# Attention on Trainium2: the next pair's scores ahead of a pair's turning, and outputs multiplied by turned reciprocal sums

## The chip, the cores and the metric

The kernel runs on one core of one Trainium2 chip. The metric is the time of one execution on the device in microseconds (us), the median of several runs. The engines are TensorE (PE, its weight loads PEld), VectorE (DVE), ScalarE (ACT), GpSimd (POOL) and SyncE (SP), which issues the transfers.

## The reference

One layer of a decoder with 1024 tokens of width 1024 in float32. An RMSNorm and one input projection feed two mixers side by side: a gated DeltaNet with 4 heads of 128, and a dilated attention with 8 heads of 64. Their outputs are joined, projected, and added to the input; a gated MLP with a short convolution follows, and a last RMSNorm.

The change lies in the attention. Every query sees keys at three dilations, and the three branches are merged by their softmax denominators, which amounts to one softmax over all keys with weights:

```
DIL_PATTERNS = ((128, 1), (512, 4), (2048, 16))
num_tot = wts[0][..., None] * nums[0] + wts[1][..., None] * nums[1] + wts[2][..., None] * nums[2]
den_tot = wts[0] * dens[0] + wts[1] * dens[1] + wts[2] * dens[2]
out = num_tot / den_tot[..., None]
```

The kernel takes the branches' weights as logarithms in a mask `mk` and makes one softmax a query: exponentials, their sum, and a weighted sum of values divided by it.

## The kernel before, in words

**Who sets the order.** The kernel is written as streams (generators) that issue instructions; a planner, the class Weave, runs them. Every stream has a level; the lowest level that says it is ready goes next. A stream yields the time that it still has to wait, which `need` (L95) works out from the planner's own prices: for VectorE 0.07 us + 0.00105 us an element, for ScalarE 0.12 + 0.00085, and 0.28 more until others see the result (L148 to L152). A product notes its result as made 0.25 later (L88 to L93). The order of TensorE's instructions is fixed by this plan: every matmul and transpose carries an issue-order token. On the other engines a scheduler orders by readiness and priority; `uv` and `ua` are VectorE and ScalarE with a raised priority.

**The streams that matter.** `dense` (L478, level 9) makes the columns of the input projection: per column two halves of 8 x 3 products of 128x512, with raw weights split into a high and a low part first (`weight`, L211: whi on ScalarE, wlo on VectorE). The order of its columns is DENSE (L42): the queries and keys of attention (`a`) stand before the gates (`z`) of the other mixer. `attention` (L892, level 5) goes ahead of dense wherever it is ready, so dense fills. `out_proj` (L1072, level 8) begins when dense has ended.

**Attention.** Four head pairs (pi), for each two halves of the tokens (hh), for each two pairs of items (u = 0, 1 and 2, 3). An item is one block of 128 queries of two heads (e = 0, 1); n = 4 hh + u is its block. It has 128 or 256 near keys and 32 (n - 1) far ones, together wd = 128 to 448 columns. For a pair:

- `scores` (L904) takes two PSUM banks of the tag asc for the first item and two of atr for the second (each tag has two banks in all), and writes queries by keys into them.
- `softmax` (L929): for each head a fused add of the mask and minimum on VectorE (the reduce; it reads the bank and writes `sm`), then the exponential on ScalarE with its sum in `den`, then the reciprocal of `den` (128x2) and a scaling of the two rows of `sm` by it.
- `turn` (L945) transposes `sm` on TensorE into a fresh bank, of asc for the first item and atr for the second, in four steps (item by head). It waits for the bank and for `sm`, less a slack (TSLACK, 1.0 us and 0.6 us, L955). VectorE copies near columns to `pt`, ScalarE far ones to `pb`.
- `values` (L966) multiplies values by `pt` into the bank `po` of the half (tag ch), `merge_classes` (L975) adds those by `pb` when the half is complete, and `give` (L989) copies `po` to SBUF with its columns put back in order, and stores it.

`advance` (L1004) is the loop: it turns the older pair, issues the new pair's scores, and then the older pair's values. The loop at L1017 loads the next head pair when its second half begins, which waits for dense to have made its queries and keys (L1021).

**Slots.** SBUF tiles come from tags with a fixed number of buffers (SLOTS, L26). The tag `dv*` takes buffers of dv and dw in turn.

Of the kernel before, what the change touches and what calls it, by code (L numbers as in the profile page):

```python
# [7 lines left out]
F32 = mybir.dt.float32  # L8
F32R = mybir.dt.float32r
AF = mybir.ActivationFunctionType  # L10
OP = mybir.AluOpType
# [11 lines left out]
APART = 0.5  # L23
KSLACK = 1.0
EPS = 1e-6
SLOTS = {"kT": 2, "kU": 2, "dv": 2, "dw": 2, "kt": 4, "uy": 5, "qa": 4, "ev": 2, "go": 2, "Xa": 7, "Xb": 9}  # L26
TURNS = {"kT*": ("kT", "kU"), "dv*": ("dv", "dw"), "X": ("Xa",) * 7 + ("Xb",) * 9}
HTAGS = ("kU", "kU", "dw", "dw", "kt", "kt", "kt", "kt", "uy", "uy", "uy", "uy", "uy", "qa", "qa", "qa", "qa",
         "ev", "ev", "go", "go") + ("Xa",) * 7
R1TAGS = ("kU", "kt", "qa", "uy", "kt", "qa", "uy", "ev", "kU", "dw", "uy")  # L30
R2TAGS = ("kt", "kt", "uy", "uy", "qa", "qa", "ev", "go", "go", "dw", "Xa")
PTAGS = ("Xb",) * 9 + ("Xa",) * 2
TOKEN = "pe"
SLACK = 3.0
# [110 lines left out]
def hybrid_layer(tc, I, out):  # L145
# [22 lines left out]
    def A(name, tag, dt=F32, shape=(P, 1024)):  # L168
        if tag in TURNS:
            i = turns[tag] = turns.get(tag, -1) + 1  # L170
            tag = TURNS[tag][i % len(TURNS[tag])]
        return tile_(lp, shape, dt, name, tag, SLOTS[tag])

# [70 lines left out]
    def bank(tag, name="ps"):  # L244
        return tile_(pp_, (P, 512), F32, name, tag, 2)
# [544 lines left out]
    def chain(h):  # L790

        for i in range(H):
            yield from wv.until(("m", i))
            yield from wv.until(("v", i))
        d = G[h]
        kT, ktok, vtok, yt, ge, rq, gq, ke = [d[n] for n in ("kT", "ktok", "vtok", "yt", "ge", "rq", "gq", "ke")]
        if not ct:
            ct.append(A("ct", "uy", shape=(P, 8, P)))
        sts = ct[0][:, 2 * h:2 * h + 2, :]
        qa = chain_load(h, 0)  # L800
        ps = bank(("asc", "ch")[h // 2])
        ms = small("ms", 4)
        tg = str(h)
        st = None
        for c in range(NCH):
            cs = slice(c * P, (c + 1) * P)
            if c == 2 and h < 2:
                qb = chain_load(h, 1)
            if c == 3 and h >= 2:
                yield from wv.until(("c", h - 2, 3))  # L810
                qb = chain_load(h, 1)
            if c == 4:
                qa = qb
            qT, at = [qa[:, i, (c % 4) * P:(c % 4 + 1) * P] for i in range(2)]
            if c == 0:
                r = vtok[:, cs]
                yield wv.need(ps, vtok, yt)
            else:
                yield wv.need(ps, st, slack=HOP)
                mm(ps[:, 0:P], kT[:, cs], st, 0.215)  # L820
                r = tile_(sp, [P, P], F32, "r", "r" + tg, 1)
                uv.scalar_tensor_tensor(r, ps[:, 0:P], ngam[:, c, h:h + 1], vtok[:, cs], op0=OP.mult, op1=OP.add)
                yield wv.need(r, slack=HOP)
            mm(ps[:, P:2 * P], yt[:, c, :], r, 0.215)
            w = tile_(sp, [P, P], F32, "w", "w" + tg, 1)
            if c < NCH - 1:
                wke = tile_(sp, [P, P], F32, "wke", "r" + tg, 1)
                uv.tensor_scalar(wke, ps[:, P:2 * P], ke[:, c:c + 1], None, op0=OP.mult)
            ua.activation(w, ps[:, P:2 * P], AF.Copy)
            if c < NCH - 1:  # L830
                yield wv.need(wke, slack=HOP)
                mm(ps[:, 2 * P:3 * P], ktok[:, cs], wke, 0.215)
                sn = sts[:, c % 2, :]
                if c == 0:
                    uv.tensor_copy(sn, ps[:, 2 * P:3 * P])
                else:
                    uv.scalar_tensor_tensor(sn, st, ge[:, c:c + 1], ps[:, 2 * P:3 * P], op0=OP.mult, op1=OP.add)
            yield wv.need(w, qa, slack=HOP)
            po = yield from next_bank("atr")
            if c:  # L840
                mm(po[:, P:2 * P], qT, st, 0.215)
            mm(po[:, :P], at, w, 0.215)

            ua.activation(vtok[:, cs], po[:, :P], AF.Copy, scale=rq[:, c:c + 1])
            if c:
                uv.scalar_tensor_tensor(vtok[:, cs], po[:, P:2 * P], gq[:, c:c + 1], vtok[:, cs], op0=OP.mult,
                                        op1=OP.add)
            if c < NCH - 1:
                st = sn
            osq = tile_(sp, [P, P], F32, "osq", "osq", 1)  # L850
            ua.activation(osq, vtok[:, cs], AF.Square, accum_out=ms[:, c:c + 1])
            wv.done.add(("c", h, c))

        ve.tensor_scalar(ms, ms, 1.0 / 128, EPS, op0=OP.mult, op1=OP.add)
        rsqrt(ms, ms, NCH)
        po_.tensor_tensor(v8(vtok), v8(vtok), ms[:, :, None].to_broadcast([P, NCH, P]), op=OP.mult)
        wv.add(1, finish(h, vtok))
# [34 lines left out]
    def attention():  # L892
# [36 lines left out]
        def softmax(it):  # L929
            pss, wd = it.pop("ps"), it["wd"]  # L930
            sm = it["sm"] = A("sm", "dv*", shape=(P, 2, 512))
            mx = tile_(sp, [P, 4], F32, "mx", "mx", 4)
            mn, den = mx[:, :2], mx[:, 2:]
            for e in range(2):
                uv.tensor_tensor_reduce(out=sm[:, e, :wd], in0=pss[e][:, :wd], in1=mk[:, 448 - wd:], scale=-0.125,
                                        scalar=-NEG, op0=OP.add, op1=OP.min, accum_out=mn[:, e:e + 1])
            for e in range(2):
                ua.activation(sm[:, e, :wd], sm[:, e, :wd], AF.Exp, bias=mn[:, e:e + 1], scale=-1.0,
                              accum_out=den[:, e:e + 1])

            uv.reciprocal(den, den)
            for e in range(2):
                uv.tensor_scalar(sm[:, e, :wd], sm[:, e, :wd], den[:, e:e + 1], None, op0=OP.mult)

        def turn(pair):  # L945
            pts = A("pt", "dv*", shape=(P, 4, 256))
            for b, (it, tag) in enumerate(zip(pair, ("asc", "atr"))):
                sm, near, far = it["sm"], it["near"], it["far"]
                nf = -(-far // P)
                it["pt"] = []  # L950
                for e in range(2):
                    pt = pts[:, 2 * b + e, :]
                    it["pt"].append(pt)
                    pp = bank(tag)
                    yield wv.need(pp, sm, slack=TSLACK[b])  # L955
                    for i in range(near // P):
                        tp(pp[:, i * P:(i + 1) * P], sm[:, e, far + i * P:far + (i + 1) * P])
                    for i in range(nf):
                        tp(pp[:, near + i * P:near + (i + 1) * P], sm[:, e, i * P:(i + 1) * P])
                    uv.tensor_copy(pt[:, :near], pp[:, :near])  # L960
                    for i in range(nf):
                        rows = min(far - i * P, P)
                        ua.activation(it["pb"][e][:rows, it["u"], i, :], pp[:rows, near + i * P:near + (i + 1) * P],
                                      AF.Copy)

        def values(pair):  # L966
            yield wv.need(pair[0]["po"], *pair[0]["pt"], slack=-PSLACK)
# [21 lines left out]
        def give(g):  # L989
            po, hh = g["po"], g["hh"]  # L990
            oT = tile_(sp, [P, 512], F32, "oT", "t2", 2)
            ve.tensor_copy(oT.rearrange("p (n u c) -> p n c u", n=4, c=4),
                           po.rearrange("p (n c u) -> p n c u", n=4, c=4))
            if g["pi"] < 3 or hh == 0:
                sy.dma_start(mixer[4 + g["pi"]][:, half(hh)], oT)
            else:
                last["oT"] = oT
            if hh == 1:
                wv.done.add(("o", 4 + g["pi"]))
# [3 lines left out]

        def advance(pair):  # L1004
            done = pipe.pop() if pipe else None
            if done is not None:
                yield from turn(done)
            if pair is not None:
                yield from scores(pair)
                pipe.append(pair)  # L1010
            if done is not None:
                yield from values(done)
                if done[1]["u"] == 3:
                    yield from merge_classes(done[0]["g"])
                    give(done[0]["g"])

        for pi in range(4):  # L1017
            q, k, vn, vc = cur
            for hh in range(2):
# [7 lines left out]
                for t in pb:  # L1027
                    for rows, b in (((slice(96, 128), 0), (slice(32, 64), 1)) if hh else ((slice(32, 64), 0),)):
                        po_.memset(t[rows, 0 if b < hh else 2, b, :], 0.0)
                g = dict(po=po, pb=pb, hh=hh, pi=pi, vc=vc)  # L1030
                for u in (0, 2):
                    yield from advance([dict(n=4 * hh + i, u=i, q=q, k=k, vn=vn, po=po, pb=pb, g=g)
                                        for i in (u, u + 1)])
# [528 lines left out]
```

## Time and profile before

| What | us |
|---|---|
| median of 3 runs | 1223.81 |
| lowest and highest run | 1223.63, 1225.67 |
| the profiled execution's own time | 1230.37 |
| its span, first to last instruction | 1228.5 |
| busy in it: TensorE, VectorE, ScalarE | 1204.7, 948.3, 571.0 |
| attention stage, first scores to first output projection product | 329.8 to 484.7 |

The mean granted TensorE clock of the profiled execution is 0.993 of full speed. Times in the trace count from the span's start. In a row of groups come the line (often a helper's: L141 is an engine call with its raised or usual priority, L189 a matmul, L193 a transpose), the engine, the operation, the tiles written and read, the shapes, the count, then busy time, mean ns of one, and the idle time in front with what ended it. In windows there are busy time and count for each engine, then the granted clock (PEclk), the share of the DMA engines and GB/s. A tile's rows have shortest, median and longest duration in ns, and the first and last start. In a timeline stand start, duration, engine, line and operation, with the idle time in front in brackets. Matmuls overlap one another: the spacing of their starts, not their duration, is what one costs.

### The profile page before, as it was taken

Reading aid. Unit: us, or ns where it says so; the run is one execution under the profiler, and the core shown is the slowest. Engines: PE = TensorE matmul, PEld = TensorE weight load, DVE = VectorE, ACT = ScalarE, POOL = GpSimd, SP = SyncE. Lnnn points to the kernel's source line nnn. Section 1 sums busy time; section 2 is a strip of 40 time slices with the busy share of each in tenths; the row PEclk is TensorE's granted clock in tenths of the full one; section 3 lists DMA queues with packets and bytes.
Section 4 is the critical chain, followed back from the end, with each engine's and each line's share of the span. In section 5 each row is a group of like instructions: output and inputs, shape, how many; then the busy total and the mean of one; then the engine's idle time right before and its main releaser. Section 6 shows DMA issues by size and latency. Waiting matters only on the chain.

```text
span 1228.5 us, 17935 instructions
## 1 busy us (share of the span) xinstructions
PE 1204.7 (98%) x6848; PEld 993.7 (81%) x6848; DVE 948.3 (77%) x1522; ACT 571.0 (46%) x1115; POOL 51.5 (4%) x58
## 2 busy tenths in 40 slices
PE   9999999999999999999999999999999999999996
PEld 7878887888877777788788888888888878787885
DVE  7675964566476778567888988889888889898875
ACT  7393344356344345555545445444444553344541
POOL 0211010003100000000000000000000000000000
PEclk9999999999999999999999999999999999999998
DMA  7325252345723303344123132231221496455523
GB/s 232 104 76 166 86 142 82 121 132 154 231 84 104 121 27 118 140 138 154 52 86 103 52 103 84 71 103 54 101 93 62 134 370 238 166 164 175 193 86 138
DMA packets 85799, 154.80 MB, mean 126 GB/s; under 512 B 21168, under 2 KB 36304, under 8 KB 85712
## 3 DMA queue, kind: packets, MB, share of 16 engines
q1 hardware_dynamic: 85712, 153.64, 38.8%
q8 instruction: 54, 0.88, 0.3%
q14 instruction: 33, 0.27, 0.1%
HBM read 117.68 MB, written 35.93 MB: 125 GB/s over the span
## 4 chain that ended last, share of the span: by engine, by line
PE 81%; DVE 8%; DMA 5%; issue 2%; ACT 2%; SPq 0%; POOLq 0%; POOL 0%; DVEq 0%; ACTq 0%
PE ps L189 42%; PE pa L189 19%; PE pc L189 9%; PE dw L189 8%; DMA wd<-in_wd 3%; PE ps L193 3%; DVE pr L139 2%; DMA r<-upark 2%; DVE wd L139 1%; DVE x1h L139 1%; DVE kT L139 1%; PE warm L189 1%; ACT dec L139 1%; DMA wst<-in_wu 0%; DVE sm L141 0%
## 5 line engine op out<-in xcount | busy, mean ns | idle before, releaser
L189 PE MATMUL dw<-pr 128*128 128x512 f32 (+1 forms) x984 | 213.4, 378 | 3.5 <-DVE x1h L139 2.3
L189 PEld LDWEIGHTS dw<-pr 128*128 128x128 f32 x984 | 176.1, 188 | 39.7 <-DVE x1h L139 4.4
L189 PE MATMUL ps<-xhi,whi 128*128 128x512 f32 x384 | 160.2, 417 | 0.0
L189 PE MATMUL ps<-xhi,wlo 128*128 128x512 f32 x384 | 150.4, 392 | 0.0
L189 PE MATMUL ps<-xlo,whi 128*128 128x512 f32 x384 | 150.2, 391 | 0.0
L189 PE MATMUL pa<-T,pair 128*128 128x512 f32 x528 | 128.7, 393 | 1.3 <-ACT u L139 1.3
L189 PEld LDWEIGHTS pa<-T,pair 128*128 128x128 f32 x528 | 100.2, 190 | 22.5 <-ACT u L139 1.6
L189 PEld LDWEIGHTS ps<-xhi,wlo 128*128 128x128 f32 x384 | 72.2, 188 | 15.7
L189 PEld LDWEIGHTS ps<-xhi,whi 128*128 128x128 f32 x384 | 72.5, 189 | 14.9 <-issue 2.6
L189 PEld LDWEIGHTS ps<-xlo,whi 128*128 128x128 f32 x384 | 72.7, 189 | 11.2
L139 ACT ACTIVATE u<-pa 128x512 f32<-128x512 f32 x44 | 26.3, 598 | 110.4 <-PE pa L189 110.4
L139 DVE SCALAR_TENSOR_TENSOR y<-xu,fcw,y 128x1023 f32<-128x1023 f32 (+1 forms) x44 | 56.4, 1281 | 25.7 <-ACT y L139 25.6
L139 ACT ACTIVATE whi<-wst 128x1024 fp32r<-128x1024 f32 (+2 forms) x42 | 43.0, 1023 | 68.8 <-PE ps L189 62.4
L189 PE MATMUL pc<-T,S 128*128 128x512 f32 x264 | 63.4, 389 | 0.0
L189 PE MATMUL pa<-B,A 128*128 128x512 f32 x264 | 63.4, 389 | 0.0
L189 PE MATMUL pc<-B,pair 128*128 128x512 f32 x264 | 63.4, 389 | 0.0
L189 PE MATMUL pa<-T,S 128*128 128x512 f32 x264 | 63.4, 389 | 0.0
L141 ACT ACTIVATE sm<-sm,mx 128x128 f32<-128x128 f32 (+7 forms) x64 | 35.5, 555 | 58.8 <-DVE mx L141 58.8
L139 DVE TENSOR_TENSOR wst<-wst 128x512 f32<-128x512 f32 x88 | 60.5, 688 | 0.8
L189 PE MATMUL ps<-B,pair 128*128 128x512 f32 x252 | 60.5, 389 | 0.0
L139 DVE TENSOR_TENSOR wlo<-wst,whi 128x1024 fp32r<-128x1024 f32 (+2 forms) x42 | 49.4, 1177 | 13.2 <-ACT whi L139 13.0
L139 ACT ACTIVATE pr<-wd 128x1024 fp32r<-128x1024 f32 x33 | 34.9, 1059 | 51.9 <-PE dw L189 23.1
(238 smaller groups left out, 2363.7 us busy)
## 6 DMA issues: line engine op xcount, KB each, us to landing
wst<-in_wu SPq DMA_DIRECT2D x44, 512.0 KB, 3.7
wd<-in_wd SPq DMA_DIRECT2D x44, 512.0 KB, 4.2
upark<-y SPq DMA_DIRECT2D x22, 512.0 KB, 3.7
wst<-in_wi SPq DMA_DIRECT2D x21, 512.0 KB, 3.7
r<-upark SPq DMA_DIRECT2D x11, 512.0 KB, 8.1
r<-upark SPq DMA_DIRECT2D x22, 256.0 KB, 7.1
wa<-in_wd SPq DMA_DIRECT2D x22, 256.0 KB, 2.7
wst<-in_wv SPq DMA_DIRECT2D x8, 512.0 KB, 3.7
```

The lines of the kernel that those rows point to most:

```text
L139: return getattr(eng, op)(*a, **kw)
L141: return getattr(eng, op)(*a, **kw)
L189: tc.stamp_issue_order_token(nc.tensor.matmul(dst, lhs, rhs, start=start, stop=stop, **kw).ins, TOKEN)
L193: tc.stamp_issue_order_token(nc.tensor.transpose(dst, src, ident).ins, TOKEN)
```

## The change

Two things in attention, and slots that go with them.

*The order.* `advance` issues the new pair's scores first, then turns the older pair, then its new step `spread`, then its values.

*The division.* `softmax` leaves the exponentials unscaled and keeps `den`. `turn` makes, for each item, a 128x128 tile `rd` whose columns are the reciprocal of the item's two sums, 64 columns for each head. `spread` transposes `rd` into a bank `rb` (tag ch, one for each half), so that every output element has its reciprocal at its own place; once the half is complete, ScalarE copies the bank to `rT`. `give` multiplies `po` by `rT` in place of the plain copy.

*Slots.* `pt` goes from `dv*` to a tag `ux` with one buffer, which `uy` gives up; the tags of some tiles of the MLP follow.

```
-SLOTS = {"kT": 2, "kU": 2, "dv": 2, "dw": 2, "kt": 4, "uy": 5, "qa": 4, "ev": 2, "go": 2, "Xa": 7, "Xb": 9}
+SLOTS = {"kT": 2, "kU": 2, "dv": 2, "dw": 2, "kt": 4, "uy": 4, "ux": 1, "qa": 4, "ev": 2, "go": 2, "Xa": 7, "Xb": 9}
...
-            ct.append(A("ct", "uy", shape=(P, 8, P)))
+            ct.append(A("ct", "ux", shape=(P, 8, P)))
...
-
-            uv.reciprocal(den, den)
-            for e in range(2):
-                uv.tensor_scalar(sm[:, e, :wd], sm[:, e, :wd], den[:, e:e + 1], None, op0=OP.mult)
+            it["den"] = den
...
         def turn(pair):
-            pts = A("pt", "dv*", shape=(P, 4, 256))
+            pts = A("pt", "ux", shape=(P, 4, 256))
             for b, (it, tag) in enumerate(zip(pair, ("asc", "atr"))):
-                sm, near, far = it["sm"], it["near"], it["far"]
+                sm, near, far, den, u = it["sm"], it["near"], it["far"], it["den"], it["u"]
+                rd = tile_(sp, [P, P], F32, "rd", ("r0", "r1", "w0", "w1")[u], 1)
+                uv.reciprocal(rd.rearrange("p (e d) -> p e d", e=2), den[:, :, None].to_broadcast([P, 2, 64]))
+                it["rd"] = rd
...
+        def spread(pair):
+            g = pair[0]["g"]
+            yield wv.need(g["rb"], *[it["rd"] for it in pair])
+            for it in pair:
+                tp(g["rb"][:, it["u"] * P:(it["u"] + 1) * P], it["rd"])
+            if pair[1]["u"] == 3:
+                g["rT"] = tile_(sp, [P, 512], F32, "rT", "t2", 2)
+                ac.activation(g["rT"], g["rb"], AF.Copy)
...
-            ve.tensor_copy(oT.rearrange("p (n u c) -> p n c u", n=4, c=4),
-                           po.rearrange("p (n c u) -> p n c u", n=4, c=4))
+            by = [t.rearrange("p (n c u) -> p n c u", n=4, c=4) for t in (po, g["rT"])]
+            ve.tensor_tensor(oT.rearrange("p (n u c) -> p n c u", n=4, c=4), *by, op=OP.mult)
...
             done = pipe.pop() if pipe else None
-            if done is not None:
-                yield from turn(done)
             if pair is not None:
                 yield from scores(pair)
                 pipe.append(pair)
             if done is not None:
+                yield from turn(done)
+            if done is not None:
+                yield from spread(done)
                 yield from values(done)
...
-                g = dict(po=po, pb=pb, hh=hh, pi=pi, vc=vc)
+                g = dict(po=po, pb=pb, hh=hh, pi=pi, vc=vc, rb=bank("ch"))
```

More of the change, by code (lines that the diff above doesn't have):

```diff
@@ L25 @@
 EPS = 1e-6
-SLOTS = {"kT": 2, "kU": 2, "dv": 2, "dw": 2, "kt": 4, "uy": 5, "qa": 4, "ev": 2, "go": 2, "Xa": 7, "Xb": 9}
+SLOTS = {"kT": 2, "kU": 2, "dv": 2, "dw": 2, "kt": 4, "uy": 4, "ux": 1, "qa": 4, "ev": 2, "go": 2, "Xa": 7, "Xb": 9}
 TURNS = {"kT*": ("kT", "kU"), "dv*": ("dv", "dw"), "X": ("Xa",) * 7 + ("Xb",) * 9}
-HTAGS = ("kU", "kU", "dw", "dw", "kt", "kt", "kt", "kt", "uy", "uy", "uy", "uy", "uy", "qa", "qa", "qa", "qa",
+HTAGS = ("kU", "kU", "dw", "dw", "kt", "kt", "kt", "kt", "uy", "uy", "uy", "uy", "ux", "qa", "qa", "qa", "qa",
          "ev", "ev", "go", "go") + ("Xa",) * 7
 R1TAGS = ("kU", "kt", "qa", "uy", "kt", "qa", "uy", "ev", "kU", "dw", "uy")
-R2TAGS = ("kt", "kt", "uy", "uy", "qa", "qa", "ev", "go", "go", "dw", "Xa")
+R2TAGS = ("kt", "kt", "uy", "ux", "qa", "qa", "ev", "go", "go", "dw", "Xa")
 PTAGS = ("Xb",) * 9 + ("Xa",) * 2
```

## The prediction

> **What bounds the kernel now.** I read the page's busy shares first, then the attention stage (329.8 to 484.7 us) in windows, then who waited in it, then one turn of its loop.
>
> ```profile
> span 1228.5 us, 17935 instructions
> PE 1204.7 (98%) x6848; PEld 993.7 (81%) x6848; DVE 948.3 (77%) x1522; ACT 571.0 (46%) x1115; POOL 51.5 (4%) x58
> ```
>
> ```profile
> core 0: us, PE busy (x) PEld busy (x) DVE busy (x) ACT busy (x) POOL busy (x), PEclk, DMA share, GB/s
> ...
> 337.87:341.28 3.41, 1.68 (x50) 1.11 (x47) 2.48 (x11) 2.10 (x8) 0.00 (x0) 1.00 0.52 204
> 341.28:344.70 3.42, 3.16 (x14) 2.69 (x13) 2.37 (x7) 0.96 (x6) 0.00 (x0) 0.50 0.00 0
> 344.70:478.50 133.80, 133.69 (x1304) 104.54 (x1304) 98.81 (x281) 57.62 (x178) 3.48 (x18) 1.00 0.27 86
> 478.50:484.70 6.20, 5.28 (x66) 4.28 (x64) 6.13 (x11) 3.46 (x10) 0.00 (x0) 1.00 0.27 70
> ```
>
> TensorE is full in the long third window: dense projection products fill whatever attention leaves. It is not full at the start (1.68 of 3.41 us, and the next 3.42 us at a granted clock of 0.50) or at the end. The waits of the stage that belong to TensorE:
>
> ```profile
> PE ps L193 <- DVE sm L141: 2.0, 2, 1.7
> ...
> PEld ps L189 <- ACT pb L141: 1.6, 4, 0.5
> PEld ps L189 <- DVE pt L141: 1.4, 2, 1.1
> ```
>
> That is 5.0 us, and the half clock took about 1.4 (half of the 3.42 less some 0.6 idle in it). So **the most that a better order can win here is 6.4 us**, 0.5% of the time. The work that the change takes off VectorE is not what the end waits for.
>
> **VectorE's exchange.** Its groups in the stage, then the other two reciprocals of the trace:
>
> ```profile
> L141 DVE CUSTOM_DVE_ANT_0 sm<-ps,mk 128x128 f32<-128x128 f32 (+7 forms) x64 | 27.9, 491 | 24.0 <-PE ps L189 24.0
> L141 DVE COPY pt<-ps 128x256 f32<-128x256 f32 (+1 forms) x64 | 23.1, 402 | 8.7 <-PE ps L193 8.6
> L141 DVE TENSOR_SCALAR sm<-sm,mx 128x128 f32<-128x128 f32 (+7 forms) x64 | 22.0, 387 | 1.1
> L139 DVE TENSOR_TENSOR wlo<-wst,whi 128x1024 fp32r<-128x1024 f32 x8 | 9.8, 1222 | 0.4 <-ACT whi L139 0.3
> L139 DVE COPY oT<-ps 128x512 f32<-128x512 f32 x8 | 8.5, 1063 | 0.0
> L139 DVE TENSOR_TENSOR aqkv<-ps,rstdB 128x512 f32<-128x512 f32 x7 | 7.6, 1082 | 3.2 <-PE ps L189 3.2
> ...
> L141 DVE RECIPROCAL mx<-mx 128x2 f32<-128x2 f32 x32 | 5.3, 165 | 4.0 <-ACT sm L141 3.4
> ```
>
> ```profile
> L139 DVE RECIPROCAL bp<-ssk x4: 203/203/203, 73.3 to 98.7; 128x8 f32<-128x8 f32 x4
> ```
>
> ```profile
> L139 DVE RECIPROCAL beta<-beta x1: 355/355/355, 40.3 to 40.3; 128x32 f32<-128x32 f32 x1
> ```
>
> Removed: 64 scalings (22.0) and 32 small reciprocals (5.3), 27.3 us. Added: 32 reciprocals of 128x128. From 8 to 32 columns the row grows by 152 ns, 6.3 ns a column; 355 + 96 x 6.3 = 960 ns (an estimate; bounds 355 ns, were the width free, and 1420 ns, four times the 32-column one), so 30.7 us. The multiply that replaces the copy of the outputs is of the kind of aqkv (1082 against 1063 ns): 8 x 0.02 = 0.2. VectorE thus has 3.6 us more to do, not less.
>
> [...]
>
> **TensorE's added work.** Sixteen transposes in a row:
>
> ```profile
> 478.48 1.91 PE L193 MATMUL ps<-ident,sm 128*128 128x128 f32 x16
> ```
>
> The last lasts 0.27, so (1.91 - 0.27) / 15 = 0.109 us each. 32 more, of the reciprocal rows: **+3.5 us** on the engine that is full. ScalarE's 8 copies of 128x512 cost 8 x 0.6 (row below) beside a 46% busy engine: nothing, and 0.6 each if its cover went.
>
> ```profile
> L139 ACT ACTIVATE u<-pa 128x512 f32<-128x512 f32 x44 | 26.3, 598 | 110.4 <-PE pa L189 110.4
> ```
>
> **The order.** One turn of the loop, a pair with 352 and 384 keys, then the reduce at other widths:
>
> ```profile
> 463.16 1.68 PE L189 MATMUL ps<-kT,qT 64*128 64x256 f32 x40
> ...
> 464.71 0.52 DVE L141 CUSTOM_DVE_ANT_0 sm<-ps,mk 128x352 f32<-128x352 f32 x1 [1.19 <-PE ps L189]
> ...
> 464.77 1.09 PE L189 MATMUL ps<-pt,vn 128*64 128x128 f32 x16
> ...
> 465.16 0.52 DVE L141 CUSTOM_DVE_ANT_0 sm<-ps,mk 128x352 f32<-128x352 f32 x1
> ...
> 466.08 0.55 DVE L141 CUSTOM_DVE_ANT_0 sm<-ps,mk 128x384 f32<-128x384 f32 x1
> ...
> 469.26 0.82 PE L193 MATMUL ps<-ident,sm 128*128 128x128 f32 x6
> ...
> 470.60 0.82 PE L193 MATMUL ps<-ident,sm 128*128 128x128 f32 x6
> ```
>
> ```profile
> L141 DVE CUSTOM_DVE_ANT_0 sm<-ps,mk 128x416 f32<-128x416 f32 x8 | 4.4, 588 | 5.5 <-PE ps L189 5.5
> ...
> L141 DVE CUSTOM_DVE_ANT_0 sm<-ps,mk 128x288 f32<-128x288 f32 x8 | 3.3, 456 | 7.9 <-PE ps L189 7.9
> ...
> L141 DVE CUSTOM_DVE_ANT_0 sm<-ps,mk 128x128 f32<-128x128 f32 x8 | 2.0, 287 | 6.1 <-PE ps L189 6.1
> ```
>
> Before, the values of the older pair follow the scores at once (464.77), and 4.5 us of mostly dense products lie ahead of the turn (469.26): nothing waits. Now the older pair's transposes follow the scores, and they need the very banks that the scores just filled (asc twice, atr twice); a bank is free when its reduce is done. Will the planner fill that gap? It prices a 352-wide reduce at 0.07 + 0.00105 x 352 = 0.44, adds 0.25 and 0.28 of hand-over, 0.97, and L955 asks for that less TSLACK's 1.0: below zero. At 416 it is 1.04, less the 0.34 that it gives the second item's far products. So no filler is put in, the four steps stand directly behind the scores, and TensorE, whose order is fixed, waits on the chip.
>
> How long: reduce k (0 to 3) of duration b ends k(b - 0.07) + b - 0.06 after the scores (starts lie 0.45 apart at b = 0.52); steps have 1 to 4 transposes of 0.109. Scores (2,3) before turn (0,1), b 0.456, steps of 1, 1, 2, 2: the last reduce ends at 1.55, the turn at 1.77, its work is 0.65, wait 1.1. Scores (4,5) before turn (2,3), b 0.521: 1.81 + 0.33 - 1.31 = 0.8. Scores (6,7), b 0.588: 2.08 + 0.33 - 1.31 = 1.1. Scores (0,1), b 0.287, before four-transpose steps: 0.2. Together 3.3 per head pair, times 4: **+13.1 us** (bounds: 0 if filled; 27 if each turn waits for a whole set of reduces, 1.7 x 16).
>
> Queued behind each wait are the values, the next scores and all dense products. The loop shortens from 9.75 us a pair (reduces run from 330.4 to 476.7 in the next row, 15 pairs) to some 6.5, since the turn no longer waits for the next softmax; dense work is then left over and runs alone, with nothing late but its own inputs.
>
> ```profile
> L141 DVE CUSTOM_DVE_ANT_0 sm<-ps,mk x64: 278/502/625, 330.4 to 476.7; 128x128 f32<-128x128 f32 x8, 128x256 f32<-128x256 f32 x8, 128x288 f32<-128x288 f32 x8, 128x320 f32<-128x320 f32 x8
> ```
>
> VectorE needs (27.9 + 23.1 + 8.7 + 30.7) / 16 = 5.65 of those 6.5. A 1.1 or 1.2 us operation of the dense stream that lies in front of a reduce delays the turn; I take a quarter of the pairs by some 0.75: **+3** (0 to 19, every pair by 1.2).
>
> Stalls that go: the first group's 2.0 and its clock 1.4, the scores' bank waits 1.6, the last values' 1.4: **-6.4** (0 to -6.4). Late next: without attention behind the last dense column, the second output weight, split in
>
> ```profile
> 478.45 1.07 ACT L139 ACTIVATE whi<-wst 128x1024 fp32r<-128x1024 f32 x1
> ...
> 480.69 1.21 DVE L139 TENSOR_TENSOR wlo<-wst,whi 128x1024 fp32r<-128x1024 f32 x1
> ```
>
> takes 2.3 and is covered by only some 1.1 of products: **+1.2** (0 to 3.6, as long as it took here). Slots (pt in ux alone, uy at 4, rd in r0 to w1) change no wait: each was last used a turn earlier. The second ch bank now holds rb, so a group's first values wait for the output multiply before, a turn (6 us) behind. No DMA is added or moved past another; the output stores come some 0.6 later, under dense work.
>
> Sum: 3.5 + 13.1 + 3 - 6.4 + 1.2 = **+14.4**. On the profiled execution (1230.37, of it 1.9 around the span) 1244.8; on the median 1223.81, which I predict, **1238.2**.
>
> **Rivals.** *The gap is filled*, because the planner sees a busier VectorE than I do: one dense step of three products (0.68) covers the first wait, and what remains is small. Then 3.5 + 1.2 - 6.4 = -1.7, 1222.1; without the late weight -2.9, 1220.9. It turns the sign once less than 1.7 us of bank waits is left over the whole stage. For it: no turn of before stalls after the first group. Chance 0.18.
>
> *The reciprocals run late.* They are ready before the scores end and VectorE idles then (24.0 us before reduces), so I put them there. If they stand behind the reduces, as written, the copies end 1.9 later per pair, of which dense pieces hide some 0.5: 15 x 1.4 = 21, 1259. In the windows 1.7 us idle in 3.41 halved the clock of the next 3.42; such waits may do that too, up to 1.7 each. [...] Chance 0.2.
>
> *The order does nothing*: old stalls stay, new ones are filled, only the transposes count: +3.5, 1227.3. Chance 0.1.
>
> The forecast keeps 0.52 (alone 1230 to 1248). The range of 1222 to 1260 takes in the third rival, the first's likelier end and nearly all of the second. A run can tell 0.2% (2.4 us): faster 0.09, same 0.11, slower 0.80.
>
> **What would show it.** Right: TensorE waiting on sm or mx at L193, some 0.2 to 1.1 after each set of scores; reciprocals near 0.96 and ahead of the reduces; reduces 6 to 7 us a pair apart; z columns after attention. Wrong: dense products between scores and transposes, or a reciprocal far from 1 us.

## The result, and the profile after

The changed kernel takes **1241.45 us** (median of 4 runs, 1240.23 to 1243.0) against 1224.74 (4 runs, 1223.63 to 1226.47): a ratio of 1.0126, with a 95% interval of 1.0105 to 1.0147. It is slower by 16.7 us in this comparison, and by 14.2 in a second one (c2_after_again, below). The prediction was 1238.2, slower, with +14.4.

Below, *before* and *after* name the two kernels' profiles, and a *group* is one half of a head pair: two turns. The head of the page of after: the span, and the busy time of each engine.

```profile
span 1238.5 us, 17942 instructions
PE 1211.1 (98%) x6880; PEld 993.3 (80%) x6880; DVE 949.0 (77%) x1458; ACT 572.4 (46%) x1123; POOL 53.0 (4%) x58
```

VectorE's busy time is the same as before (949.0 against 948.3), and TensorE still fills 98%. The loss is found in the attention stage, which now lasts from 328.92 to 497.04, 168.1 us in place of 154.9. Its windows (busy time and count of each engine, then the granted clock, DMA share, GB/s):

```profile
333.00:335.96 2.96, 1.12 (x36) 0.52 (x34) 2.96 (x9) 0.85 (x3) 0.00 (x0) 1.00 0.47 183
335.96:339.37 3.41, 3.35 (x11) 2.76 (x12) 3.04 (x8) 1.39 (x6) 0.00 (x0) 0.50 0.43 149
339.37:463.00 123.63, 117.93 (x1272) 87.01 (x1270) 85.61 (x217) 52.80 (x187) 3.40 (x18) 1.00 0.25 76
463.00:497.04 34.04, 34.04 (x166) 28.21 (x164) 19.33 (x19) 9.11 (x9) 0.00 (x0) 1.00 0.20 57
```

Two things are to be seen. In the third row TensorE lacks 5.7 of 123.6 us, where before it lacked 0.1 of 133.8. And attention ends at 463, some 21 us earlier than before, but what the loop saved is not won: in the last row dense products run alone for 34 us. Who waited in the stage (engine, tile and line, then what it waited for, us in total, times, the longest):

```profile
PEld ps L193 <- DVE mx L141: 12.1, 34, 0.8
...
PE ps L193 <- DVE mx L141: 7.0, 12, 1.7
...
PEld ps L189 <- DVE pt L141: 4.0, 11, 0.4
PEld ps L189 <- DVE rd L141: 1.5, 4, 0.4
```

The transposes of line 193 wait for `mx`, the result of the last part of a reduce (a row of its own of 77 to 85 ns; for the first reduce of the turn below it stands at 350.06), that is for the bank that the reduce still reads. The waits of weight loads and of products overlap, so I measure TensorE's loss by the **starts of its products**: one that follows scores starts 0.2 us later when nothing holds it (the middle of 0.15 to 0.31, by the form of the scores, in c1_before_again), a transpose 0.109 after a transpose, a dense product 0.227 after a dense product (each lasts 0.39); what is above that is a wait. Sums made so are good to some 0.5 us. One turn in the timeline of after (start, duration):

```profile
347.88 1.89 PE L189 MATMUL ps<-kT,qT 64*128 64x256 f32 x40
...
349.54 0.59 DVE L141 CUSTOM_DVE_ANT_0 sm<-ps,mk 128x416 f32<-128x416 f32 x1 [0.37 <-PE ps L189]
...
350.06 0.58 DVE L141 CUSTOM_DVE_ANT_0 sm<-ps,mk 128x416 f32<-128x416 f32 x1
350.19 0.31 PEld L193 LDWEIGHTS ps<-ident,sm 128*128 128x128 f32 x3 [0.80 <-DVE mx L141]
350.20 2.15 PE L193 MATMUL ps<-ident,sm 128*128 128x128 f32 x12 [0.42 <-DVE mx L141]
...
350.71 0.31 PEld L193 LDWEIGHTS ps<-ident,sm 128*128 128x128 f32 x3 [0.20 <-DVE mx L141]
...
351.25 0.31 PEld L193 LDWEIGHTS ps<-ident,sm 128*128 128x128 f32 x3 [0.23 <-DVE mx L141]
...
351.80 0.31 PEld L193 LDWEIGHTS ps<-ident,sm 128*128 128x128 f32 x3 [0.23 <-DVE mx L141]
...
352.33 0.94 DVE L141 RECIPROCAL rd<-mx 128x128 f32<-128x128 f32 x1
```

No dense product stands between the scores and the turn. Each of the four steps (three transposes) starts when one more of the four reduces has ended: 350.19, 350.71, 351.25, 351.80, the spacing of the reduces. The twelve transposes are 1.3 us of work and take 1.9. The page counts pipelined transposes from the first to the last, so they look busy: the windows show less of this than the starts do.

All 15 turns that have scores ahead of them stand so, and but for the first each kind of pair repeats to a few hundredths of a us:

| Scores, then turn | Turns | Wait of one, forecast | Wait of one, measured |
|---|---|---|---|
| (2,3), then (0,1), first group | 1 | 1.1 | 2.63 |
| (2,3), then (0,1), the others | 3 | 1.1 | 1.33 |
| (4,5), then (2,3) | 4 | 0.8 | 1.07 (once 1.01) |
| (6,7), then (4,5) | 4 | 1.1 | 1.22 |
| (0,1), then (6,7) | 3 | 0.2 | 0.18 |
| all | 15 | 13.1 (for 16 turns) | 16.3 |

With 0.1 behind the very first scores, which dense products follow, the sum is 16.4. Before, the same sums are 0.4 behind scores and 1.5 within turns; some 0.9 of the latter is transposes at the half clock, as is some 0.3 of the first turn's 2.63.

Why the first turn waits 1.3 longer than its kind is to be seen on VectorE. The scores ahead of it begin at 332.05, but the first reduce that frees a bank starts at 334.63 only, behind two wide reciprocals and two operations of the dense stream (`aqkv` and `wlo`):

```profile
330.80 1.94 DVE L141 RECIPROCAL rd<-mx 128x128 f32<-128x128 f32 x2
332.65 1.00 DVE L139 TENSOR_TENSOR aqkv<-ps,rstdB 128x512 f32<-128x512 f32 x1
333.51 1.19 DVE L139 TENSOR_TENSOR wlo<-wst,whi 128x1024 fp32r<-128x1024 f32 x1
334.63 0.43 DVE L141 CUSTOM_DVE_ANT_0 sm<-ps,mk 128x288 f32<-128x288 f32 x1
```

The new operations of VectorE, by tile (ns shortest/median/longest, first and last start), and the reduces:

```profile
L141 DVE RECIPROCAL rd<-mx x32: 935/942/954, 330.8 to 456.4; 128x128 f32<-128x128 f32 x32
```

```profile
L139 DVE TENSOR_TENSOR oT<-ps,rT x8: 1078/1090/1094, 348.1 to 463.8; 128x512 f32<-128x512 f32 x8
```

```profile
L141 DVE CUSTOM_DVE_ANT_0 sm<-ps,mk x64: 285/503/621, 329.5 to 453.8; 128x128 f32<-128x128 f32 x8, 128x256 f32<-128x256 f32 x8, 128x288 f32<-128x288 f32 x8, 128x320 f32<-128x320 f32 x8
```

The reciprocal of 128x128 takes 942 ns (estimated 960), the output multiply 1090 (1082).

### The profile page after: what moved, and what is told of

Its sections match the earlier page's. It is cut to its first block, busy times and chain, and to the rows that moved or that the text cites. A ratio compares the mean times of both kernels' runs of the same rounds, so it can differ in the third digit from the quotient of the medians.

```text
span 1238.5 us, 17942 instructions
## 1 busy us (share of the span) xinstructions
PE 1211.1 (98%) x6880; PEld 993.3 (80%) x6880; DVE 949.0 (77%) x1458; ACT 572.4 (46%) x1123; POOL 53.0 (4%) x58
## 4 chain that ended last, share of the span: by engine, by line
PE 81%; DVE 8%; DMA 5%; issue 3%; ACT 2%; SPq 0%; POOL 0%; POOLq 0%; DVEq 0%; ACTq 0%
PE ps L189 42%; PE pa L189 19%; PE pc L189 9%; PE dw L189 7%; PE ps L193 4%; DMA wd<-in_wd 2%; DVE pr L139 2%; DVE x1h L139 1%; DVE wd L139 1%; DMA r<-upark 1%; DVE kT L139 1%; ACT dec L139 1%; DVE wlo L139 1%; DMA xt<-in_xT 1%; DVE r L139 0%
## 5 line engine op out<-in xcount | busy, mean ns | idle before, releaser
L189 PEld LDWEIGHTS ps<-xhi,whi 128*128 128x128 f32 x384 | 72.6, 189 | 13.7 <-issue 1.7
L139 DVE TENSOR_TENSOR wlo<-wst,whi 128x1024 fp32r<-128x1024 f32 (+2 forms) x42 | 49.4, 1177 | 13.1 <-ACT whi L139 13.0
```

Source lines behind the costliest of these rows:

```text
L139: return getattr(eng, op)(*a, **kw)
L189: tc.stamp_issue_order_token(nc.tensor.matmul(dst, lhs, rhs, start=start, stop=stop, **kw).ins, TOKEN)
```

## The experiments

The theory: the order makes TensorE wait for the banks behind the scores, and this is most of the loss. The rivals: the division costs it (VectorE's 942 ns operations late, or the added transposes); the planner leaves the gap because it prices the wide reciprocal too low; the first group's stall and half clock of before are chance and not the kernel's. None of these kernels leaves out a part of the reference. "Stage" is the time from the first scores to the first output projection product; "waits" are the excess of starts behind scores, within turns and within values.

| Run | Median us | Ratio to before (95%) | Stage | Waits |
|---|---|---|---|---|
| c1_before_again | 1225.96, one run | | 155.31 | 0.4 / 1.3 / 1.5 |
| c2_after_again | 1239.79 | 1.0130 (1.0113 to 1.0147) | 168.07 | 8.3 / 8.1 / 0.2 |
| e1_order | 1232.83 | 1.0048 (1.0033 to 1.0064) | 159.30 | 6.3 / 5.2 / 0 |
| e2_division | 1228.86 | 1.0021 (1.0011 to 1.0030) | 155.84 | 0.4 / 0.9 / 0 |
| e3_fill | 1232.15 | 1.0044 (1.0029 to 1.0059) | 156.92 | 0.4 / 0.1 / 3.1 |
| e4_small_rd | 1240.24 | 1.0110 (1.0095 to 1.0125) | 165.98 | 7.8 / 8.0 / 0 |
| e5_order_fill | 1223.41 | 0.9984 (0.9972 to 0.9996) | 150.65 | 0.5 / 0.9 / 0 |
| e6_true_price | 1242.87 | 1.0142 (1.0124 to 1.0160) | 169.37 | 7.7 / 8.5 / 0 |
| e7_double_spread | 1244.06 | 1.0141 (1.0125 to 1.0157) | 173.00 | 8.3 / 8.1 / 1.3 |
| e8_swapped_banks | 1249.07 | 1.0183 (1.0168 to 1.0198) | 177.22 | 21.1 / 3.6 / 0.5 |
| e9_fill_small_rd | 1225.87 | 0.9998 (0.9989 to 1.0008) | 152.47 | 0.4 / 0.1 / 0 |

The kernel before had medians of 1226.64 (beside e1 to e4), 1225.57 (c1, c2, e5, e6) and 1226.26 (e7 to e9).

Two things are not in these columns. In e1 and in e5 one turn behind a dense step still waited for its bank, 0.8 and 1.1 us. And the stages of before, after, c1, c2, e7 and e8 hold a stretch of 3.41 us at half clock, worth 1.6; those of the others hold none.

### The parts alone: e1_order and e2_division

e1 takes the division back (small reciprocal, scalings, plain copy of the outputs) and keeps the order and the slots:

```
-            it["den"] = den
+            uv.reciprocal(den, den)
+            for e in range(2):
+                uv.tensor_scalar(sm[:, e, :wd], sm[:, e, :wd], den[:, e:e + 1], None, op0=OP.mult)
...
-            if done is not None:
-                yield from spread(done)
```

> Order alone: scores before the turn, the division as before (small reciprocals, probabilities scaled), pt in its own slot. Theory (the turn's transposes wait for banks that the scores hold): 13 of 15 turns still stand directly behind scores, only the 32 transposes (3.5 us) are gone, so some 10 to 13 us over before, 1235 to 1238. Rival (the wide reciprocals or the added transposes are what costs): no slower than before, 1222 to 1227.

Measured: +6.2 us, below the theory's range and above the rival's. The sign is the theory's, the size is not. Its waits explain that: they are there (below), but 11.5 us in place of 16.4, because the planner now starts only 13 turns straight behind scores and puts a dense step of three products into the middle of five of them. The waits of e1, then one split turn in its timeline:

```profile
PEld ps L193 <- DVE mx L141: 14.3, 33, 1.1
...
PE ps L193 <- DVE mx L141: 5.8, 12, 0.7
```

```profile
351.24 1.06 PE L193 MATMUL ps<-ident,sm 128*128 128x128 f32 x6 [0.42 <-DVE mx L141]
352.06 0.48 PE L189 MATMUL ps<-xhi,whi 128*128 128x512 f32 x1
...
352.83 0.81 PE L193 MATMUL ps<-ident,sm 128*128 128x128 f32 x6
```

The first six transposes wait, the second six, behind three dense products, don't (0.81 is their undisturbed time). Why the plan differs was only argued, not shown: in e1 the older pair's scalings stand in the planner's queue for VectorE.

e2 takes the order back and keeps the division:

```
+            if done is not None:
+                yield from turn(done)
             if pair is not None:
...
-                yield from turn(done)
-            if done is not None:
                 yield from spread(done)
```

> Division alone: turned reciprocals and the multiply at the end, the order as before (turn, scores, values). Theory: the 32 transposes cost 3.5 us, few turns stand behind scores, so 3 to 8 us over before, 1228 to 1233. Rival (reciprocals of 0.94 us load VectorE): most of the loss stays, 1236 or more.

Measured: 1228.86, in the range; the stage is 0.5 us longer than that of c1. By the starts, the 32 transposes cost 5.6 here, since each pair of them stands between scores and values, with a change of 0.2 of its own. Against that go 1.6 of the first group's wait, 1.9 of other waits, and a half clock worth 1.6 (c1 has it in its attention stage, e2 does not): 5.6 - 1.6 - 1.9 - 1.6 = 0.5 (some 0.6 of the 1.9 is transposes at the half clock, so counted twice, and the sum is no closer than that). So the division and the new slots, which e2 keeps, make by themselves none of the waits behind the scores.

Alone the parts give +4.0 and +0.5 in the stage, and both in one kernel (c2) +12.8. Going from e1 to c2 the stage grows by 8.8: 4.3 more waits (16.6 against 11.5 and the 0.8 behind a dense step), 2.5 for the transposes (by the starts a pair among dense products adds 0.155, 16 pairs, some 0.3 of it at the half clock), 1.6 for a half clock that c2 has and e1 has not; that is 8.4, about what is found. The parts are not independent, because each makes a plan of its own.

### The wait covered: e3_fill, e5_order_fill, e9_fill_small_rd

e3 is after, with a planner that asks for the whole wait of the turn:

```
-TSLACK = -1.0, -0.6
+TSLACK = 0.0, 0.0
```

> The changed kernel with TSLACK 0.0, 0.0 in place of -1.0, -0.6: the planner puts one or two dense steps (three products, 0.68 us) between scores and transposes in 14 of 15 turns, nothing else changes. Theory: bank waits are covered, 12 us or more come back, 1226 to 1231. Rival (VectorE is the bound): the time stays within 3 us of the changed kernel, 1238 to 1244.

Measured: 1232.15, 1.2 above the range. The waits behind scores and in turns are gone (0.5 us in place of 16.4), and the stage is 11.2 shorter than after's; 1.6 of that is the half clock. The filler has a price: the second product of a block of dense products starts some 0.32 after the first, in place of 0.227, and e3 has 55 such blocks where after has 35, which costs 2.2. And the loss has a second face. The waits of e3:

```profile
PEld ps L189 <- DVE pt L141: 5.7, 14, 0.7
PE ps L189 <- DVE pt L141: 1.1, 3, 0.5
```

There is no row for `mx` any more; now the values wait for `pt`, 3.1 us by the starts. VectorE makes the wide reciprocal between the reduces and the last copies, in the timeline of e3:

```profile
345.93 0.93 DVE L141 RECIPROCAL rd<-mx 128x128 f32<-128x128 f32 x1
346.78 0.36 DVE L141 COPY pt<-ps 128x256 f32<-128x256 f32 x1
347.20 0.65 PE L189 MATMUL ps<-pt,vn 128*64 128x128 f32 x6 [0.43 <-DVE pt L141]
```

e9 is e3 with the reciprocal taken of 128x2 and widened by ScalarE:

```
-                uv.reciprocal(rd.rearrange("p (e d) -> p e d", e=2), den[:, :, None].to_broadcast([P, 2, 64]))
+                uv.reciprocal(den, den)
+                ac.activation(rd.rearrange("p (e d) -> p e d", e=2), den[:, :, None].to_broadcast([P, 2, 64]), AF.Copy)
```

> The changed kernel with TSLACK 0.0, 0.0 as in e3 and the reciprocal on the two sums as in e4. In e3 the values waited some 3 us in all, behind copies that stand after reciprocals. Theory: with bank waits covered VectorE's 0.94 us reciprocals do count, these 3 us go, 1.5 to 4 us below e3, 1227 to 1231. Rival (the values wait for something else): as e3, 1232.

Measured: 1225.87, better than expected by 1.1, and not to be told from before. The stage is 4.4 shorter than e3's, 3.1 of it in the values, which wait no more by the starts, and 1.0 in the products by `pb` behind them. The row for `pt` shrinks to

```profile
PEld ps L189 <- DVE pt L141: 1.4, 5, 0.4
```

e5 is e1 with half of the first item's slack taken away:

```
-TSLACK = -1.0, -0.6
+TSLACK = -0.5, -0.6
```

> Order alone with TSLACK -0.5, -0.6: a dense step now stands between scores and transposes in 12 of 15 turns. Theory: of the 11 us of waits of the order alone some 6 to 8 go, so 1224 to 1229, close to or below the kernel before, which has 5 us of its own waits in the stage. Rival (the order costs something else too): no better than the order alone, 1231 or more.

Measured: 1223.41 (10 runs, 1222.55 to 1225.19), 0.6 below the range: a ratio of 0.9984 (0.9972 to 0.9996). **This version beats both kernels**, by 2.0 us against before (0.5 to 3.4). A turn in its timeline, to lay beside that of after:

```profile
349.86 1.89 PE L189 MATMUL ps<-kT,qT 64*128 64x256 f32 x40
...
351.51 0.59 DVE L141 CUSTOM_DVE_ANT_0 sm<-ps,mk 128x416 f32<-128x416 f32 x1 [0.43 <-PE ps L189]
351.68 0.50 PE L189 MATMUL ps<-xhi,whi 128*128 128x512 f32 x1
...
352.49 0.82 PE L193 MATMUL ps<-ident,sm 128*128 128x128 f32 x6
...
353.06 0.48 PE L189 MATMUL ps<-xhi,whi 128*128 128x512 f32 x1
...
353.84 0.82 PE L193 MATMUL ps<-ident,sm 128*128 128x128 f32 x6
```

Three dense products lie ahead of each half of the turn, and both halves take 0.82, as a set of six does undisturbed. The stage is 4.7 shorter than c1's: the first group's wait (1.8), its half clock (1.6) and the values' wait (1.5) are gone, 4.9 together. Against them stands the one turn that still waits 1.1 (its transposes start at 432.60): two VectorE operations, the output copy of 1.07 us and an `og` of 1.22, run ahead of its first reduce (432.10). In the stage this is most of the 6.4 that the prediction named as the most to be won by order; of the whole time less is won, since e5 has a half clock behind the stage, at 583.12, which c1 has not (spans of 1220.8 and 1224.1).

### VectorE and the planner's price: e4_small_rd, e6_true_price

e4 is after with e9's edit of the reciprocal, and the slack of after.

> The changed kernel with the reciprocal taken on the two sums (128x2) and spread to 128x128 by a ScalarE copy, so that VectorE loses 32 operations of 0.94 us and gains 32 of 0.17. Theory: the first wait of each turn stays; only VectorE's share of the loss goes, 1236 to 1242. Rival (the reciprocals are what costs): 1231 or less.

Measured: 1240.24, in the range. VectorE is relieved (926.0 busy in place of 949.0), and the waits of the turns stay:

```profile
PEld ps L193 <- DVE mx L141: 12.1, 34, 0.8
...
PE ps L193 <- DVE mx L141: 6.5, 12, 1.2
```

All 14 later turns wait as in after, to 0.01. The 2.1 by which the stage is shorter than c2's lie in the first group alone: its turn waits 0.7 less, and no half clock follows.

e6 prices the reciprocal in the plan by what it takes:

```
-            us = 0.3 + 0.165 * n if kw.get("op") == OP.pow else fixed + per * n
+            us = 0.3 + 0.165 * n if kw.get("op") == OP.pow else 0.15 + 0.0063 * n if op == "reciprocal" else fixed + per * n
```

> The changed kernel with the planner told that a reciprocal of n columns takes 0.15 + 0.0063 n us (0.96 at 128, it believes 0.20). Transposes still stand directly behind scores in 14 of 15 turns; two more dense steps go between turn and values. Theory: the bank waits stay, at most the small waits of the values go, 1237 to 1242. Rival (the plan is wrong because the reciprocal is mispriced): 1232 or less.

Measured: 1242.87, 0.9 above the range, and no gain. The waits of e6:

```profile
PEld ps L193 <- DVE mx L141: 10.7, 30, 0.8
...
PE ps L193 <- DVE mx L141: 7.5, 12, 1.4
```

One turn, at 449.86, waits 3.1 in place of 1.1: three operations of the dense stream (`wlo`, `zz` and `og`, 1.2 us each) stand ahead of and among its reduces. The price of the reciprocal is not what leaves the gap open. That rival falls.

### The suspects made larger: e8_swapped_banks, e7_double_spread

e8 has the first item turn into the bank that the scores filled last. The greater slack keeps TensorE's order nearly as it is (in three turns the dense step between the turn and the transposes of `rd` goes elsewhere):

```
-TSLACK = -1.0, -0.6
+TSLACK = -2.5, -2.5
...
-            for b, (it, tag) in enumerate(zip(pair, ("asc", "atr"))):
+            for b, (it, tag) in enumerate(zip(pair, ("atr", "asc"))):
```

> The changed kernel with the turn's banks swapped: the first item's transposes go to atr, which the third and fourth reduce free, the second item's to asc (and TSLACK -2.5, -2.5, which keeps TensorE's order as it was). Theory (the transposes wait for the bank's reduce): the first wait behind the scores grows by two reduces, some 0.9 us, the waits within the turn shrink, 0.4 to 0.8 a turn in all, 1246 to 1253. Rival (they wait for the softmax or for the reciprocals): 1239 to 1243.

Measured: 1249.07, in the range. The waits of e8:

```profile
PE ps L193 <- DVE mx L141: 19.7, 15, 2.5
PEld ps L193 <- DVE mx L141: 18.1, 19, 1.9
```

Little changes but the bank that a step needs, and the waits by the starts grow from 16.4 to 24.7 (+8.3), the stage by 9.2, the time against before from 14.2 to 22.8. A wait of these banks goes into the time about one for one.

e7 makes each transpose of the reciprocals twice:

```
-                tp(g["rb"][:, it["u"] * P:(it["u"] + 1) * P], it["rd"])
+                for _ in range(2):
+                    tp(g["rb"][:, it["u"] * P:(it["u"] + 1) * P], it["rd"])
```

> The changed kernel with each of the 32 transposes of reciprocal rows done twice. Theory: 32 more at 0.08 to 0.11 us on a full TensorE, 2.6 to 3.5 us over the changed kernel, 1242 to 1245. Rival (TensorE has room there because it waits anyway): no change.

Measured: 1244.06, in the range. The medians put it 17.8 above its before, where c2 is 14.2 above; the ratios (1.0141 and 1.0130) stand closer and their intervals overlap, so the time alone does not price the 32 more transposes. The stage does: it is 4.9 longer than c2's, 3.7 of it between transposes of `rd` (0.116 for each one added) and 1.1 of values that wait. A set of four in e7's timeline:

```profile
353.98 0.60 PE L193 MATMUL ps<-ident,rd 128*128 128x128 f32 x4
```

### The same kernels again: c1_before_again, c2_after_again

> The kernel before, unchanged, for a second profile of it: the first profiled execution took 1230.4 us beside a median of 1223.8. If its first-group stall and its two stretches of half clock are chance, this one has others and an attention stage 2 to 3 us shorter than 154.9; if they belong to the kernel, the same.

> The changed kernel, unchanged, on the chip of these runs: 1240 to 1243, some 1.2% over the kernel before, with 15 waits behind the scores again and VectorE's reciprocals at 0.94 us.

c2 fell just below its range (1239.79). Windows of c1 around its first group, then those of c2:

```profile
339.16:342.57 3.41, 1.26 (x14) 0.81 (x10) 3.05 (x15) 2.48 (x9) 0.00 (x0) 1.00 0.25 99
342.57:345.98 3.41, 3.25 (x11) 2.89 (x12) 1.49 (x5) 0.83 (x4) 0.00 (x0) 0.50 0.00 0
```

```profile
333.33:336.75 3.42, 1.64 (x42) 0.91 (x39) 3.42 (x8) 1.00 (x4) 0.00 (x0) 1.00 0.38 152
336.75:340.17 3.42, 3.31 (x12) 2.59 (x12) 3.24 (x10) 1.58 (x6) 0.00 (x0) 0.50 0.56 155
```

The stall of the first group and the half clock behind it came back in both kernels. A second half clock of the profile before, at 587.04 and outside attention, did not come back in c1; it is worth at most 1.7 (half of 3.41) of the 4.4 us by which the profiled execution before was longer than c1 (spans of 1228.5 and 1224.1). It did come in e3, e4, e5, e6 and e9, at 583.12 to 600.39, so the spans of these runs hold it too.

## Why the prediction was right, by its own steps

The order, the sign and the size were right: the planner left the gap open, and TensorE waits at line 193. That the sum came out so near is luck in part: its terms were wrong by up to 3.5 us, and the errors cancelled. The span of c1 to that of c2, 1224.1 to 1237.8, +13.7:

| Step | Forecast | Measured |
|---|---|---|
| waits behind scores | +13.1 | +16.6 (16.4, and 0.2 of the values) |
| dense operations ahead of a reduce | +3 | one turn, 1.3 with the reciprocals (in the row above) |
| transposes | +3.5 | +2.5 |
| old stalls gone | -6.4 | -5.0, and a half clock again |
| late second output weight | +1.2 | 0 |
| other spacing in the stage (what remains) | | -1.3 |
| after the stage | | +0.9 |

- **Waits behind scores.** The forecast took 3.3 for a head pair; the four kinds of turn measure 3.8 (1.33 + 1.07 + 1.22 + 0.18). The working, reduce after reduce, was right to a quarter of a us for each kind, though it took the duration of the narrower item for all four reduces. The first turn stands out, with 2.63.
- **VectorE in the way.** The mechanism came, but its size and place were wrong. I took a quarter of the pairs to be hit by 1.1 us operations of the dense stream. The waits of each kind agree to some 0.06 in all groups but the first, so one turn of 15 was hit: the first, by 1.3, where two wide reciprocals stand in the row as well (e4, without them, waits 0.7 less there). Other plans were hit in other places: e1 by 0.8, e5 by 1.1, e6 by 2.0. In the sum, the 0.5 a head pair that the term above lacked made up for the rest.
- **Old stalls.** The step that failed most: of "the first group's 2.0 and its clock 1.4" the clock did not go, and the 2.0 was replaced. In c1 a turn of the first group waits 2.0 us (1.8 above the usual spacing) for `sm`, its own softmax; that wait went. But the turn that now stands behind scores there waits 2.63 for `mx`, its bank, and the clock was halved again behind it (335.96 in after, 336.75 in c2). The forecast counted this turn among the four of its kind, at 1.1; in the first group VectorE is late, busy 2.96 of 2.96 us in the first window of after. What went beside is 3.2 of other waits. The forecast also read the clock's share too low: TensorE was busy for 3.16 of that window's 3.42 us, so it is worth 1.6, not 1.4.
- **Transposes.** 32 cost 2.5 rather than 3.5 (0.08 each), because most of them are pairs among dense products, and a transpose leaves to a dense product after 0.03. In e2, between scores and values, the same 32 cost 5.6.
- **The late weight** did not come: the first output projection product starts 0.23 after the last dense one. The 34 us of dense products alone left VectorE and ScalarE time to split it ahead.
- **Reciprocals.** Their length was right, their place right in the first turn alone (330.80): in all others they don't run ahead of the reduces but behind them, among the copies (352.33 in the turn shown). So the place of the second rival was right, and its price, 21 us, was not: in after dense steps cover nearly all (the values wait 0.2 by the starts). Where the bank waits were covered by a plan with more fill, the wide reciprocal cost 4.4 of the stage (e3 against e9).
- **The first rival**, a gap that the planner fills, is e3, made by hand: +5.5 against its before and not -1.7, mostly because it left out that the reciprocals would then hold the values; e9, where they don't, stands at -0.4. **The order does nothing** is refuted by e1.
- **The loop** came to 8.3 us a pair ((453.8 - 329.5) / 15), not 6.5: the plan put long runs of dense products between some head pairs, while the next group's inputs were made. That is no loss in itself, as the dense work had to be done in any case.
- **Half clocks behind each wait** did not come: the granted clock is 1.00 in the whole third window of after.

The -1.3 of other spacing is only a remainder, but most of it can be named: c1 has 44 blocks of dense products and c2 has 35, and the late second products of these blocks add up to 4.1 and 3.0 us. The +0.9 after the stage is less than the 1.6 by which after and c2, the same kernel, differ there (741.4 and 739.8 us). What remains open is what makes the planner split turns in e1 and not in after.

## What to carry to other kernels

When a step is moved to stand right behind another on an engine whose order is fixed, ask which buffer it re-uses, who still reads that, and in what sequence: the wait is the reader's chain of operations, piece by piece, and, where the reader is not late with other work, can be worked out to a few tenths. A slack that a plan was given for one order (here 1.0 us against a wait of 0.97) hides the new wait from it, so it has to be set again with the order; three products of filler ahead of the moved step turned a loss of 6.2 us (e1) into a gain of 2.0 (e5). And an operation that costs nothing while another wait covers it can become the next bound once that wait is mended.

## What the hardware showed

A wide reciprocal on VectorE was paid by the column: 166 ns for 2 columns, 203 for 8, 355 for 32, 942 for 128, so (942 - 355) / 96 = 6.1 ns a column from 32 on. Widening 128x2 on ScalarE to 128x128 took a copy of 293 ns instead (e4).

TensorE's granted clock was 0.50 for one stretch of 3.41 us (3.42 in c2) behind a stretch as long in which it had been busy for 1.64 (c2) or 1.26 (c1), with a single gap of 1.7. In e8 a gap of 1.48 us, ahead of 353.20, was followed by dense products of 0.39 to 0.48 us, while those that lie wholly in the half clock of c2 took 0.63 to 0.78. In e4, whose first turn waited 0.7 less (a gap of 1.16; 2.17 busy of the 3.40 us from 332.00 on), and in e5, with no gap at that place (16.00 busy of the 16.00 us from 327.00 on), the clock stayed at 1.00 (from 330 to 480 in e4, through the stage in e5).

The half clock at 583 to 600 us lies near a stretch where TensorE, between two wide products, makes only 16 products of one column. In before these take 583.87 to 585.71, with 0.77 idle behind them; from 583.63 to 587.04 TensorE was busy for 2.64 of 3.41 us, and from 587.04 to 590.45 the clock was 0.50. In after they take 596.80 to 598.64, with 0.33 idle behind them, and the clock stayed at 1.00. In e5 the 3.42 us ahead of 583.12 were busy for 3.31, and yet the next 3.41 had a clock of 0.50. So the busy time of the stretch ahead (2.17 of 3.40 in e4, with no half clock behind it) does not tell by itself whether the half clock comes, and what decides it is not shown.
